# Weight subtractions hung behind their copies, phase work split around the low parts, and a later combination in a one-core attention and S5 kernel

## The chip, the core and the metric

The kernel runs on one core of a Trainium2 chip. The metric is the time of one execution on the device, in microseconds. The runs of the kernel before gave a median of 3143.69 us (3 runs, 3141.63 to 3149.01).

## What is computed

The reference is a trunk of two layers over a prompt of 1024 and a sample of 512 tokens, with 1024 channels, in float32. The kernel takes both together as 1536 tokens, 12 tiles of 128. Layer 0, with which this change deals, is attention with three head groups of different window and dilation and a SiLU gate; layer 1 is a bidirectional S5 (state space) layer. For layer 0 the core is:

```python
xqkvz = h @ w_in            # h: normed and modulated x; 1024 -> 3*3*1024 + 1024
for g, (window, dil) in enumerate(((128, 1), (512, 4), (2048, 16))):
    q, k, v = rope(q_g), rope(k_g), v_g        # 16 heads of 64
    o_g, lse_g = dilated_window_attention(q, k, v, dil, radius)
w = softmax over g of lse_g                    # the combination
y = (sum_g w_g * o_g) * silu(z) @ w_out
```

This is a shortened paraphrase of the reference's loop. The S5 layer needs tables of powers of complex numbers, computed from its parameters alone; the kernel makes them during layer 0 ("prep").

## The kernel before, in words

**Units and items.** The 16 heads are taken as 8 pairs p. A unit (p, g) is the input projection of one pair in one group, with g = 3 for the gate. The order is (0,0) to (7,0), and then (p,1), (p,2), (p,3) for p = 0 to 7. A unit with g < 3 has 12 items T, one for each tile of 128 tokens; an item is 24 matmuls of 128x384 (`gemm`, L876 to L888): 8 pieces k of the contraction, and for each piece hi by hi, hi by lo and lo by hi, since every float32 factor is split into a rounded high part and the rest. A g = 3 unit has 3 items of 24 matmuls, 512 wide. Matmuls 3k to 3k+2 of an item need the weights of piece k, the second of them the low half.

**The order of work.** `Timeline` (L90 to L114) holds the items and hooks. Before each of the 24 matmuls, and at the end (slots 0 to 24), it issues the hooks that were registered for (item, slot), in the order of registration. So a slot only fixes the place of an instruction in the in-order queue of its engine; engines run as far ahead as their operands allow. A slot of 25 or more is carried into the next items.

**Stages of an item.** After item T, at slot 24, `stage_rope` multiplies q and k by cos and sin on DVE (L914, L915) and adds the parts on POOL (L898, L899). In the next item ACT copies the value's high parts at slot 3 (L941) and DVE makes the low parts at slot 7 (L894). At slot 13 PE transposes q and k (L950, L951), at slot 16 ACT copies their high parts (L963, L965), at slot 18 DVE makes the low parts, "the qk lows" (L968, L970), and POOL copies halves of kT (L974). Scores come two items later (L994, L998), then the maximum and exponential (L1021, L1024, L1009), the transposes of the exponentials (L1042, L1052, L1054), and the product with the values (L1067), added up by ACT and POOL (L1076, L1077, L1081).

**Weights of the next unit.** `w_dma` (L824) fetches a piece into one of two buffers (wraw), from SP's queue. `w_cvt` (L837 to L844) takes one of 11 buffers (whl), copies the high part on ACT (L842) and subtracts on DVE for even k and on POOL for odd k (L843). `attention` (L692 to L782) hooks copy and subtraction together, for g < 3 at slot 16 of items 2, 4, 6 (k0 to k2), at slots 5, 6, 18 and 22 of the last item T = 11 (k3 to k6), and at slot 6 of the next unit's first item (k7). The fetch of piece k+2 follows at the same slot, since it takes the buffer of piece k. A g = 3 unit gives k its slot 19 + 6k, and the fetch 20 + 6k. Sixteen units of 12 items are followed by a unit with eight pieces (seven times g = 0 by g = 0, (7,0) by (0,1), and g = 1 by g = 2 for each of the 8 pairs); those with g = 2 are followed by the gate, which has four pieces of 256 columns.

**Combination.** At the end of (p, 2) the three groups' statistics are stored and read back (`combine_load`, L1109). `combine_prep` (L1114 to L1143) makes the factors: part 0 on DVE and ACT (L1122 to L1126), part 1 on DVE (to L1134), and part 2 transposes them on PE (L1138), copies them (L1140), stores them (L1141) and fetches them spread over the partitions as f (L1152). `combine` (L1155) begins two items later by multiplying f (L1164).

**S5 tables.** `prep_hooks` (L1361) lays one eighth of the tables beside each of seven g = 0 units, (0,1), and each g = 2 unit. `prep_tab` are POOL operations of 128x512 (L1252 to L1262) at slots 8 and 19 of items 2 to 4 and 6 to 8. `prep_phase` (L1324 to L1359), with j = 0 to 6 in items 2 to 8, doubles a table of phases: part 0 is three DVE operations (L1346 to L1348), part 1 three more (L1350 to L1352), on up to 128x252 elements, all operands in SBUF.

```python
            for k in range(n):
                i, sl = [(first + 2, 16), (first + 4, 16), (first + 6, 16), (last, 5), (last, 6), (last, 18), (last, 22), (last + 1, 6)][k]
                H(i, sl, self.w_cvt, nu, k)
                ...
                if k + 2 < n:
                    H(i, sl, self.w_dma, nu, k + 2)
```

Of the kernel before, what the change touches and what calls it, by code (L numbers as in the profile page):

```python
# [10 lines left out]
F32 = mybir.dt.float32  # L11
F32R = mybir.dt.float32r
BF = mybir.dt.bfloat16
I32 = mybir.dt.int32
AF = mybir.ActivationFunctionType
ALU = mybir.AluOpType
# [11 lines left out]
NW = 11  # L28
# [112 lines left out]
class Kern:  # L141
# [157 lines left out]
    def startup(self):  # L299


        nc, I = self.nc, self.I
# [100 lines left out]
        self.s5_some(3.4)  # L403
        for T in range(2):
            self.x_scale(T)
        self.w_cvt(unit, 0, True)
        self.w_cvt(unit, 1, True)
        for i in range(8):
            if i < 3:
                piece_load(i + 5)  # L410
# [24 lines left out]
            if i in (5, 7):  # L435
                self.to_hm(None, 2, 0, S, None, (i - 3) // 2)
            for k in ((2,), (3,), (), (4,), (5,), (6,), (7,), ())[i]:
                self.w_cvt(unit, k, True)
            if i > 0:
                multiply(i - 1)  # L440
            if i < 7:
# [250 lines left out]
    def attention(self):  # L692
# [10 lines left out]
        for u, (p, g) in enumerate(units):  # L703
            first = at_unit[p, g] = len(tl.items)
            n = NT if g < 3 else 3
            for T in range(n):
# [5 lines left out]
                if g < 3:  # L712
                    end = u + 2 == len(units)
                    early = u == 0 and T == 0
                    at = {"rope": (0, 24), "qk": (2, 2) if early else divmod(38, 25), "scores": divmod(76, 25), "soft": divmod(79, 25), "et": divmod(100, 25), "pv": divmod(118, 25)}
                    if end:
                        at.update(LAST.get(T, {}))
                    end_of = 0
                    for nm, (ds_, sl) in at.items():

                        ds_, sl = at[nm] = divmod(max(25 * ds_ + sl, end_of), 25)
                        end_of = 25 * ds_ + sl + max((0, *LATER.get(nm, ()))) + 1
                        H(i + ds_, sl, getattr(self, "stage_" + nm), p, g, T)
                        for part, d in enumerate(LATER.get(nm, ())):
                            H(i + ds_ + (sl + d) // 25, (sl + d) % 25, getattr(self, "stage_" + nm), p, g, T, part + 1)
                    if T == NT - 1:
                        st = divmod(25 * at["soft"][0] + at["soft"][1] + LATER["soft"][0], 25)
                        H(i + st[0], st[1], self.stats_out, p, g)
                        if g == 0:
                            H(i + at["pv"][0] + (at["pv"][1] + LATER["pv"][1] + 1) // 25, (at["pv"][1] + LATER["pv"][1] + 1) % 25, self.u0_store, p)  # L730
                        if end:
                            H(i + st[0], st[1], self.combine_load, p)
                            for k, sl in enumerate((4, 10, 16)):
                                H(i + 3, sl, self.combine_prep, p, k)
                        elif g == 2:
                            H(i + st[0], st[1], self.combine_load, p)
                            for k, sl in enumerate((10, 16, 24)):
                                H(i + 4, sl, self.combine_prep, p, k)
                            for c in range(3):
                                for k, (ds_, sl) in enumerate(((0, 10), (0, 22), (1, 14), (1, 24))):  # L740
                                    H(i + 6 + 3 * c + ds_, sl, self.combine, p, c, k)
                            H(i + 16, 2, self.u0_load, p + 1)
                elif u + 1 < len(units) or T < n - 1:
                    H(i, 24, self.stage_silu, p, T)
            last = i
            if u + 1 == len(units):
                continue
            nu = units[u + 1]
            if g == 3:
                for k in range(8):  # L750
                    H(first + (19 + 6 * k) // 25, (19 + 6 * k) % 25, self.w_cvt, nu, k)
                    if k < 2:
                        H(first, 3, self.w_dma, nu, k)
                    if k < 6:
                        H(first + (20 + 6 * k) // 25, (20 + 6 * k) % 25, self.w_dma, nu, k + 2)
                continue
            n = 8 if nu[1] < 3 else 4
            for k in range(n):
                i, sl = [(first + 2, 16), (first + 4, 16), (first + 6, 16), (last, 5), (last, 6), (last, 18), (last, 22), (last + 1, 6)][k]
                H(i, sl, self.w_cvt, nu, k)  # L760
                if k < 2:
                    H(first, 3, self.w_dma, nu, k)
                if k + 2 < n:
                    H(i, sl, self.w_dma, nu, k + 2)

        second = at_unit[0, 1]
        starts = [12 + 11 * k for k in range(7)] + [second] + [at_unit[p, 2] for p in range(npairs)]
# [66 lines left out]
            nc.sync.dma_start(raw, W[256 * k:256 * k + 256, 9216 + 128 * p:9344 + 128 * p].rearrange("(k p) n -> p k n", p=128))  # L834
        self.raw[(unit, k)] = raw

    def w_cvt(self, unit, k, start=False):  # L837

        nc, g = self.nc, unit[1]
        raw = self.raw.pop((unit, k))  # L840
        w = self.sb(self.pools["A"], [128, 2, 384] if g < 3 else [128, 2, 2, 128], F32R, "whl", bufs=NW)
        nc.scalar.activation(w[:, 0], raw, AF.Copy)  # L842
        (nc.gpsimd if start or k in (1, 3, 5, 7) else nc.vector).tensor_tensor(w[:, 1], raw, w[:, 0].bitcast(F32), op=ALU.subtract)  # L843
        self.wt[(unit, k)] = w  # L844

    @staticmethod
    def tok_cols(g, T):
# [513 lines left out]
    def prep_hooks(self, b, i):  # L1361
# [13 lines left out]
        H(i + 9, 0, self.prep_b_out, b, 0)  # L1375
        H(i + 9, 20, self.prep_b_out, b, 1)
        for j in range(7):
            H(i + 2 + j, 18, self.prep_phase, b, j, 0)
            H(i + 2 + j, 22, self.prep_phase, b, j, 1)


    ADA = [(0, 2 * D), (0, 2 * D + 512)] + [(1, 512 * k) for k in range(6)]
# [641 lines left out]
```

## Time and profile before

| | |
|---|---|
| median of the runs | 3143.69 us (3141.63 to 3149.01) |
| the profiled execution's own time | 3140.71 us |
| its span in the profile | 3138.9 us |
| mean granted TensorE clock | 0.976 of full speed |
| TensorE (PE) busy | 89% |
| VectorE (DVE) busy | 68% |
| ScalarE (ACT) busy | 54% |
| GpSimd (POOL) busy | 52% |

The profile is one execution. The busy shares are means over stages: start to about 55 us, the g = 0 units to 792, (0,1) to 893.6, (0,2) to 973.2, then seven rounds of g = 3, 1, 2 to 2251, and the rest of the program, with the S5 layer, to the end. In a row of a timeline the first number is the start in us from the beginning of the span and the second the duration; "x6" is the number of like instructions drawn together, and the bracket gives the idle time of the engine before the row and what ended it.

### The profile page before, as it was taken

The numbers are of one execution on the slowest core, as the hardware profiler recorded it, in microseconds if no ns is written. First come the engines' busy times: TensorE is split into PE (matmuls) and PEld (weight loads), VectorE is DVE, ScalarE is ACT, GpSimd is POOL, SyncE is SP. The second block draws the span as 40 slices with busy tenths as digits, with TensorE's granted clock in tenths as the row PEclk, the third lists the DMA queues.
The fourth block names the chain that finished last, engine by engine and source line by source line (L and its number), as shares of the span: only waits on it lengthen the run. The fifth ranks groups of instructions, "written<-read, shape, count | busy, mean of one in ns | idle before, by whom it ended". The sixth has DMA issues, their size and how long they took to land. (4 is left out here: it accounts for less than half of the span.)

```text
span 3138.9 us, 52520 instructions
## 1 busy us (share of the span) xinstructions
PE 2788.1 (89%) x16181; PEld 2419.8 (77%) x16181; DVE 2131.3 (68%) x6071; ACT 1700.8 (54%) x5120; POOL 1620.9 (52%) x2657
## 2 busy tenths in 40 slices
PE   6799999998898888888888888889899989889998
PEld 5788888887787878878787887878678666667887
DVE  7777777776875766657575766757654799984345
ACT  5867666677665665656565665656544222223221
POOL 3655555554754554545464554545464466552343
PEclk8999999999899999999999999999999999999999
DMA  7122222221222222221222212222444555436553
GB/s 207 47 76 86 85 80 83 73 86 49 61 69 57 62 51 60 55 67 42 73 54 54 67 44 60 53 62 58 132 138 121 166 186 163 153 132 178 171 154 128
DMA packets 428232, 293.78 MB, mean 94 GB/s; under 512 B 140288, under 2 KB 379152, under 8 KB 427824
## 3 DMA queue, kind: packets, MB, share of 16 engines
q1 hardware_dynamic: 427808, 290.16, 32.3%
q8 instruction: 129, 2.11, 0.3%
q14 instruction: 151, 1.24, 0.1%
q10 hardware_dynamic: 144, 0.26, 0.0%
HBM read 204.72 MB, written 85.62 MB: 92 GB/s over the span
## 5 line engine op out<-in xcount | busy, mean ns | idle before, releaser
L885 PE MATMUL mm<-whl,hp 128*128 128x384 f32 x4584 | 992.0, 353 | 5.1 <-ACT hp L356 2.8
L885 PEld LDWEIGHTS mm<-whl,hp 128*128 128x128 f32 x4584 | 804.1, 196 | 22.2 <-issue 12.0
L885 PE MATMUL mm<-whl,hs 128*128 128x384 f32 x2304 | 498.6, 350 | 0.0
L885 PEld LDWEIGHTS mm<-whl,hs 128*128 128x128 f32 x2304 | 398.1, 192 | 7.5 <-issue 7.2
L968 DVE SCALAR_TENSOR_TENSOR qT<-qkT,qT 64x128 fp32r<-64x128 f32 x576 | 166.4, 289 | 304.1 <-ACT kT L965 297.9
L974 POOL CAST kT<-kT 64x128 fp32r<-64x128 f32 x576 | 171.2, 297 | 316.9 <-ACT kT L965 297.3
L1654 PE MATMUL mm<-hp,wi 128*128 128x512 f32 x1104 | 279.4, 401 | 2.6 <-ACT sig L1691 2.6
L1009 ACT ACTIVATE e<-e,st 128x128 f32<-128x128 f32 (+2 forms) x576 | 249.3, 434 | 52.4 <-DVE st L1024 48.4
L1081 POOL TENSOR_TENSOR u<-u,pw 128x128 f32<-128x128 f32 x384 | 188.7, 491 | 167.8 <-ACT u L1077 152.1
L950 PE MATMUL qkT<-ident,t 128*128 128x128 f32 x288 | 89.5, 311 | 184.4 <-POOL t L899 182.3
L1654 PEld LDWEIGHTS mm<-hp,wi 128*128 128x128 f32 x1104 | 202.7, 188 | 53.7 <-issue 8.6
L963 ACT ACTIVATE qT<-qkT 64x128 fp32r<-64x128 f32 x576 | 155.9, 271 | 153.6 <-PE qkT L951 146.2
L1076 ACT ACTIVATE pw<-pv 64x256 f32<-64x256 f32 x576 | 217.5, 378 | 36.2 <-PE pv L1067 25.5
L898 POOL TENSOR_TENSOR t<-t,t 128x128 f32<-128x128 f32 x288 | 137.8, 478 | 187.2 <-DVE t L915 180.2
L950 PEld LDWEIGHTS qkT<-ident,t 128*128 128x128 f32 x288 | 40.7, 141 | 241.5 <-POOL t L899 238.5
L941 ACT ACTIVATE vs<-mm 64x128 fp32r<-64x128 f32 (+1 forms) x350 | 95.6, 273 | 225.6 <-DVE t L915 223.0
L843 POOL TENSOR_TENSOR whl<-wraw,whl 128x384 fp32r<-128x384 f32 (+1 forms) x116 | 113.8, 981 | 139.9 <-ACT whl L842 138.5
L843 DVE TENSOR_TENSOR whl<-wraw,whl 128x384 fp32r<-128x384 f32 (+1 forms) x108 | 85.0, 787 | 138.5 <-ACT whl L842 138.0
L970 DVE TENSOR_TENSOR kT<-qkT,kT 64x128 fp32r<-64x128 f32 x576 | 166.3, 289 | 9.8
L1054 DVE TENSOR_TENSOR et<-eT,et 128x512 fp32r<-128x512 f32 (+1 forms) x288 | 163.5, 568 | 6.6 <-ACT et L1052 6.3
L1081 POOL TENSOR_TENSOR U<-U,pw 128x128 f32<-128x128 f32 x192 | 90.7, 472 | 147.6 <-ACT U L1077 140.1
L1067 PE MATMUL pv<-et,vs 128*128 128x256 f32 x704 | 147.8, 290 | 19.6 <-DVE et L1054 17.6
(368 smaller groups left out, 6395.0 us busy)
## 6 DMA issues: line engine op xcount, KB each, us to landing
wraw<-in_attn_w_in SPq DMA_DIRECT2D x192, 192.0 KB
par<-par_d SPq DMA_DIRECT2D x64, 512.0 KB
f<-f_d SPq DMA_DIRECT2D x44, 384.0 KB
par_d<-zs SPq DMA_DIRECT2D x64, 256.0 KB
U<-in_ada_w SPq DMA_DIRECT2D x16, 768.0 KB
par_d<-f SPq DMA_DIRECT2D x64, 128.0 KB
raw<-in_ssm_w_in SPq DMA_DIRECT2D x14, 512.0 KB
u_d<-u SPq DMA_DIRECT2D x8, 768.0 KB
```

Of the source, the lines that this page charges most:

```text
L843: (nc.gpsimd if start or k in (1, 3, 5, 7) else nc.vector).tensor_tensor(w[:, 1], raw, w[:, 0].bitcast(F32), op=ALU.subtract)
L885: nc.tensor.matmul(ps[:, :384], self.hv(a, k, self.tok_cols(g, T)), self.wt[((p, g), k)][:, b], start=m == 0, stop=m == 23)
L963: nc.scalar.activation(qT[r, h], tp[r, 0:128], AF.Copy, scale=-0.125)
L968: nc.vector.scalar_tensor_tensor(qT[o, h], tp[r, 0:128], -0.125, qT[r, h].bitcast(F32), op0=ALU.mult, op1=ALU.subtract)
L970: nc.vector.tensor_tensor(kT[r, 1, h, c], tp[r, 128:256], kT[r, 0, h, c].bitcast(F32), op=ALU.subtract)
L974: nc.gpsimd.tensor_copy(kT[o, 0, h, c], kT[r, 0, h, c].bitcast(F32))
L1009: nc.scalar.activation(e[:, h, :W], e[:, h, :W], AF.Exp, scale=-1.0, bias=st[:, T, h, 0:1], accum_out=st[:, T, h, 1:2])
L1054: nc.vector.tensor_tensor(et[:, 1, 0:n], tp[:, 0:n], et[:, 0, 0:n].bitcast(F32), op=ALU.subtract)
L1067: nc.tensor.matmul(pv[:, h], V[key][:, 2 * h:2 * h + 2].rearrange("p a c -> p (a c)"), et[:, :, ci, h], start=ci == 0, stop=ci == len(chun ...
L1076: nc.scalar.activation(w[hi], pv[hi, h], AF.Copy)
L1081: nc.gpsimd.tensor_tensor(u, u, w[:, a], op=ALU.add)
L1654: nc.tensor.matmul(st["ps"], state[("w", u)][a][:, k], self.hv(b, k, slice(512 * c, 512 * c + 512)), start=m == 0, stop=m == 23)
```

## The change

The helper that copies and subtracts a piece of weights is split in two parts, the copy (part 0) and the subtraction (part 1). At start both are still called together, all subtractions on POOL. In a unit with g < 3, k0 to k2 are copied at slot 16 of items 2, 4, 6 as before, and subtracted at slot 10 of the item behind. With L the first slot of the last item, k3 to k7 are copied at L + 4, 7, 19, 22 and 34 (before: 5, 6, 18, 22 and 31), and subtracted at L + 9, 12, 24, 27 and 39. In a g = 3 unit the copies come at 15 + 7k and the subtractions at 19 + 7k. The fetch of piece k+2 is issued behind the subtraction of piece k.

The three parts of the combination's factors, at slots 10, 16 and 24 of one item, come at slots 10 and 20 of it and 10 of the next. The phase parts, at slots 18 and 22, come at 9 and 20.

```diff
--- before.py
+++ after.py
@@ -403,8 +403,8 @@
         self.s5_some(3.4)
         for T in range(2):
             self.x_scale(T)
-        self.w_cvt(unit, 0, True)
-        self.w_cvt(unit, 1, True)
+        self.w_cvt(unit, 0)
+        self.w_cvt(unit, 1)
         for i in range(8):
             if i < 3:
                 piece_load(i + 5)
@@ -435,7 +435,7 @@
             if i in (5, 7):
                 self.to_hm(None, 2, 0, S, None, (i - 3) // 2)
             for k in ((2,), (3,), (), (4,), (5,), (6,), (7,), ())[i]:
-                self.w_cvt(unit, k, True)
+                self.w_cvt(unit, k)
             if i > 0:
                 multiply(i - 1)
             if i < 7:
@@ -734,8 +734,8 @@
                                 H(i + 3, sl, self.combine_prep, p, k)
                         elif g == 2:
                             H(i + st[0], st[1], self.combine_load, p)
-                            for k, sl in enumerate((10, 16, 24)):
-                                H(i + 4, sl, self.combine_prep, p, k)
+                            for k, sl in enumerate((110, 120, 135)):
+                                H(i + sl // 25, sl % 25, self.combine_prep, p, k)
                             for c in range(3):
                                 for k, (ds_, sl) in enumerate(((0, 10), (0, 22), (1, 14), (1, 24))):
                                     H(i + 6 + 3 * c + ds_, sl, self.combine, p, c, k)
@@ -746,22 +746,20 @@
             if u + 1 == len(units):
                 continue
             nu = units[u + 1]
+
             if g == 3:
-                for k in range(8):
-                    H(first + (19 + 6 * k) // 25, (19 + 6 * k) % 25, self.w_cvt, nu, k)
-                    if k < 2:
-                        H(first, 3, self.w_dma, nu, k)
-                    if k < 6:
-                        H(first + (20 + 6 * k) // 25, (20 + 6 * k) % 25, self.w_dma, nu, k + 2)
-                continue
+                at_w = [(15 + 7 * k, 19 + 7 * k) for k in range(8)]
+            else:
+                L = 25 * (last - first)
+                at_w = [(66, 85), (116, 135), (166, 185), (L + 4, L + 9), (L + 7, L + 12), (L + 19, L + 24), (L + 22, L + 27), (L + 34, L + 39)]
             n = 8 if nu[1] < 3 else 4
             for k in range(n):
-                i, sl = [(first + 2, 16), (first + 4, 16), (first + 6, 16), (last, 5), (last, 6), (last, 18), (last, 22), (last + 1, 6)][k]
-                H(i, sl, self.w_cvt, nu, k)
                 if k < 2:
                     H(first, 3, self.w_dma, nu, k)
+                for part in range(2):
+                    H(first + at_w[k][part] // 25, at_w[k][part] % 25, self.w_cvt, nu, k, part)
                 if k + 2 < n:
-                    H(i, sl, self.w_dma, nu, k + 2)
+                    H(first + at_w[k][1] // 25, at_w[k][1] % 25, self.w_dma, nu, k + 2)
 
         second = at_unit[0, 1]
         starts = [12 + 11 * k for k in range(7)] + [second] + [at_unit[p, 2] for p in range(npairs)]
@@ -834,14 +832,17 @@
             nc.sync.dma_start(raw, W[256 * k:256 * k + 256, 9216 + 128 * p:9344 + 128 * p].rearrange("(k p) n -> p k n", p=128))
         self.raw[(unit, k)] = raw
 
-    def w_cvt(self, unit, k, start=False):
+    def w_cvt(self, unit, k, part=None):
 
         nc, g = self.nc, unit[1]
-        raw = self.raw.pop((unit, k))
-        w = self.sb(self.pools["A"], [128, 2, 384] if g < 3 else [128, 2, 2, 128], F32R, "whl", bufs=NW)
-        nc.scalar.activation(w[:, 0], raw, AF.Copy)
-        (nc.gpsimd if start or k in (1, 3, 5, 7) else nc.vector).tensor_tensor(w[:, 1], raw, w[:, 0].bitcast(F32), op=ALU.subtract)
-        self.wt[(unit, k)] = w
+        raw = self.raw[unit, k]
+        if part != 1:
+            w = self.wt[(unit, k)] = self.sb(self.pools["A"], [128, 2, 384] if g < 3 else [128, 2, 2, 128], F32R, "whl", bufs=NW)
+            nc.scalar.activation(w[:, 0], raw, AF.Copy)
+        if part != 0:
+            w = self.wt[(unit, k)]
+            (nc.gpsimd if part is None or k in (1, 3, 5, 7) else nc.vector).tensor_tensor(w[:, 1], raw, w[:, 0].bitcast(F32), op=ALU.subtract)
+            del self.raw[unit, k]
 
     @staticmethod
     def tok_cols(g, T):
@@ -1375,8 +1376,8 @@
         H(i + 9, 0, self.prep_b_out, b, 0)
         H(i + 9, 20, self.prep_b_out, b, 1)
         for j in range(7):
-            H(i + 2 + j, 18, self.prep_phase, b, j, 0)
-            H(i + 2 + j, 22, self.prep_phase, b, j, 1)
+            H(i + 2 + j, 9, self.prep_phase, b, j, 0)
+            H(i + 2 + j, 20, self.prep_phase, b, j, 1)
 
 
     ADA = [(0, 2 * D), (0, 2 * D + 512)] + [(1, 512 * k) for k in range(6)]
```

## Rows read from the trace of the kernel before

**Rows 1.** the page, section 1: span, and busy time of TensorE
```profile
span 3138.9 us, 52520 instructions
...
PE 2788.1 (89%) x16181; PEld 2419.8 (77%) x16181; DVE 2131.3 (68%) x6071; ACT 1700.8 (54%) x5120; POOL 1620.9 (52%) x2657
```

**Rows 2.** busy time in stretches, core 0: us, PE (x), PEld, DVE, ACT, POOL, PEclk, DMA, GB/s
```profile
55.00:792.00 737.00, 652.91 (x4229) 585.38 (x4227) 543.46 (x1778) 523.17 (x1587) 409.76 (x739) 0.97 0.26 73
...
973.20:2251.00 1277.80, 1116.34 (x6725) 1023.95 (x6724) 836.67 (x2832) 786.96 (x2647) 652.35 (x1246) 0.98 0.23 57
```

**Rows 3.** waits over the whole span: engine, line, releaser: us in total, times, longest
```profile
PE qkT L950 <- POOL t L899: 182.3, 149, 3.3
...
DVE whl L843 <- ACT whl L842: 138.0, 85, 5.1
```

**Rows 4.** groups of PE, 973.2 to 2251: busy us, mean ns, idle before, releasers
```profile
L950 PE MATMUL qkT<-ident,t 128*128 128x128 f32 x169 | 52.4, 310 | 117.8 <-POOL t L899 117.1
...
L1138 PE MATMUL qkT<-ident,cd 128*72 128x128 f32 x8 | 2.8, 350 | 18.9 <-DVE cd L1134 18.9
```

**Rows 5.** waits of PE, 55 to 792
```profile
PE qkT L950 <- POOL t L899: 46.6, 46, 3.2
...
PE sc L998 <- DVE kT L970: 16.8, 15, 3.3
```

**Rows 6.** timeline of DVE, item T7 of (3,2): start, us, operation, [idle before, releaser]
```profile
1486.40 0.59 DVE L968 SCALAR_TENSOR_TENSOR qT<-qkT,qT 64x128 fp32r<-64x128 f32 x2 [1.30 <-ACT kT L965]
...
1487.61 0.57 DVE L1346 TENSOR_TENSOR f<-f,p_pb 128x128 f32<-128x128 f32 x1
...
1489.63 0.29 DVE L1352 TENSOR_TENSOR f<-f 128x128 f32<-128x128 f32 x1
```

**Rows 7.** timeline of POOL, the same item
```profile
1484.66 1.29 POOL L1256 TENSOR_TENSOR zs<-zs 128x512 f32<-128x512 f32 x1
```

**Rows 8.** timeline of PE, the same item
```profile
1491.77 0.33 PE L950 MATMUL qkT<-ident,t 128*128 128x128 f32 x1 [1.69 <-POOL t L899]
```

**Rows 9.** timeline of DVE: subtractions at the boundary (3,1) to (3,2) and in its T2
```profile
1431.65 1.42 DVE L843 TENSOR_TENSOR whl<-wraw,whl 128x384 fp32r<-128x384 f32 x1
...
1437.05 0.56 DVE L843 TENSOR_TENSOR whl<-wraw,whl 128x384 fp32r<-128x384 f32 x1 [2.22 <-ACT whl L842]
...
1453.08 0.43 DVE L843 TENSOR_TENSOR whl<-wraw,whl 128x256 fp32r<-128x256 f32 x1 [2.15 <-ACT whl L842]
```

**Rows 10.** timeline of POOL, the boundary (3,1) to (3,2)
```profile
1431.64 1.01 POOL L843 TENSOR_TENSOR whl<-wraw,whl 128x384 fp32r<-128x384 f32 x1
...
1439.82 0.45 POOL L899 TENSOR_TENSOR t<-t,t 128x128 f32<-128x128 f32 x1
```

**Rows 11.** timeline of SP's queue, the same boundary: the fetch of k7
```profile
1437.13 0.37 SPq L831 DMA_DIRECT2D wraw<-in_attn_w_in  x1
```

**Rows 12.** timeline of ACT, the same boundary: the copy of k7
```profile
1439.62 0.52 ACT L842 ACTIVATE whl<-wraw 128x384 fp32r<-128x384 f32 x1 [0.65 <-DMA wraw<-in_attn_w_in]
```

**Rows 13.** timeline of PE, the same boundary: the last six matmuls of T0
```profile
1441.72 1.21 PE L885 MATMUL mm<-whl,hp 128*128 128x384 f32 x6
```

**Rows 14.** timelines of PE and POOL at the boundaries to (6,0) and (7,2)
```profile
607.09 2.12 PE L885 MATMUL mm<-whl,hp 128*128 128x384 f32 x6
...
2155.61 0.46 POOL L899 TENSOR_TENSOR t<-t,t 128x128 f32<-128x128 f32 x1
...
2157.51 1.21 PE L885 MATMUL mm<-whl,hp 128*128 128x384 f32 x6
```

**Rows 15.** busy time in stretches, behind L950 at two boundaries (columns of rows 2)
```profile
1258.00:1261.40 3.40, 3.40 (x14) 3.40 (x13) 1.16 (x4) 2.86 (x13) 1.58 (x3) 0.51 0.48 54
...
1440.40:1443.80 3.40, 3.40 (x23) 3.37 (x24) 1.76 (x6) 3.17 (x13) 1.72 (x4) 1.00 0.33 51
```

**Rows 16.** timelines of SP's queue and DVE: factors of the combination of p = 3
```profile
1543.42 0.34 SPq L1141 DMA_DIRECT2D f_d<-ft  x1
...
1551.17 1.10 DVE L1164 TENSOR_TENSOR f<-f,u 128x512 f32<-128x512 f32 x1 [1.13 <-DMA f<-f_d]
```

## The prediction

> **What bounds the kernel now.** I read the busy shares first. TensorE works 2788.1 us, 89% of a span of 3138.9 [rows 1], so some 351 us of its idle time is all that a reordering can win. The table by stages says where it idles: 84 us from 55 to 792, where the g = 0 units run, 161 us in the seven rounds of g = 1, 2, 3 from 973 to 2251 [rows 2]. Nothing of the change lies behind 2251. The list of waits then names the last releaser. PE waits 182.3 us before the qk transposes L950 for the rope sum on POOL (L899), and DVE stands 138.0 us in front of its weight subtractions L843 until ACT has made the copy [rows 3]. The second is a wait of an engine that isn't the bound and counts only where something that PE needs is queued behind it. So I read PE alone, by stage. Of the 117.8 us before L950 in the rounds, and 18.9 before the combine transpose L1138 [rows 4], most lie in g = 2 units; in the g = 0 stage it is 46.6 before L950 and 16.8 before the scores for the low half of kT on DVE [rows 5].
>
> One item of (3,2) shows the loop. DVE makes the qk lows from 1486.40, then six phase operations from 1487.61 to 1489.92, and only then rope [rows 6]; POOL sums; PE gets L950 at 1491.77 after 1.69 us idle [rows 8]. The loop L950, ACT copies, lows, phase, rope, sum is longer than PE's own item by just that. DVE had waited 1.30 us ahead of the lows [rows 6], and the change moves phase work into that gap.
>
> **Phase work moved (prep_phase part 0 to slot 9, part 1 to slot 20).** It runs in ten items of each g = 2 unit, of seven g = 0 units and of (0,1). In the item shown 2.31 us stand between lows and rope. Part 0 took about 1.65 of it and part 1 .85. Part 1 stays behind the lows, part 0 goes before them. If part 0 fits into the gap of 1.30 the loop loses up to that. What speaks against the full gain: POOL's table operations hold slots 8 and 19, the first of this item 1.29 us from 1484.66 [rows 7]. Part 0's first operation (two SBUF inputs) took .57 beside such an operation, and part 1's last .29 when POOL was free [rows 6]. The same shows in the subtractions: .56 alone at 1437.05, 1.42 at 1431.65 beside POOL's own of 1.01 at 1431.64 [rows 9, 10]. At slot 9 part 0 starts half a microsecond into the first table operation, at slot 20 part 1 runs beside the second and POOL's additions behind it, so part 1 is now the long one (1.65 instead of .85) and part 0 spills some .4 us over the gap: in this item about 0 is won (1.65 - .80 - .85), in the item behind, with 128x252 operands, about .6. In T5, without a table operation, nothing stalls today.
>
> The Trainium skill, "SBUF — State Buffer", section "Who interferes with whom", says that a DVE instruction with two SBUF inputs contends with a GpSimd instruction that reads SBUF, and that the other fully blocks. The trace agrees as far as 1.42 = .56 + most of 1.01 goes; taken strictly over a whole part it makes a rival below.
>
> **Subtractions moved (w_cvt part 1).** In T2 of this unit DVE stands 2.15 us for the copy and subtracts .43 (1453.08) right ahead of the lows [rows 9]. The copy stands behind ACT's own qk copies, so the lows come .46 later than they could, the step to the next operation counted. After the change the subtraction comes ten slots behind the lows, in time that DVE has. I take .75 in T2 and .85 in T6 together with their small phase operations.
>
> Sum for a g = 2 unit: -.75 (T2), +.1 (T3, POOL's subtraction nearer the rope), -.85 (T6), 0 (T7), -.6 (T8): -2.1, by eight units -17, and 1 us of clock (below): **-18**. Bounds: .5 per unit (only the subtractions) and 6.3 (all that moves is hidden in T2, T3, T6, T7 and T8: 1.36 + .81 + 1.54 + 1.3 + 1.3, each the smaller of the time moved and the stall that is there), thus -4 and -50.
> In g = 0 units the lows freed of the subtraction take away most of the scores' 16.8 [rows 5], I take 11, and phase the same share of 46.6 as 18 + 7 are of 117.8 (21%): 10. **-21**; bounds -10 and -31. In g = 1 units no phase work runs, the subtractions are freed in front of the lows of T4 and T6: .9 each, **-7** (bounds -3 and -9). (0,1): **-2** (0 to -5).
>
> **Combination later.** Part 0 stays at (4,10), part 2 (L1138) goes from (4,24) to (5,10). Its wait of 18.9 [rows 4] shrinks as PE first does ten matmuls more. But f, which DVE needs at L1164, comes 7.75 us after the store L1141 (1543.42 to 1551.17) and is already waited for there by 1.13 [rows 16]. L1140 and L1141 now stand behind rope and value lows on DVE, some .8 us later, and PE arrives earlier: what is saved at L1138 is waited for two items later, DVE's lows behind L1164. With the subtraction of k0 gone from that item and about 1 us less in g = 3 units, where the subtraction held the et lows, I take **0** (bounds -8 and +8).
>
> **What it costs: the last weights of the next unit.** Only two wraw buffers exist, so piece k7 is fetched after k5's subtraction, which goes from slot 18 of the last item to slot 24, on POOL behind L1081 and L898/L899. Before: issue at 1437.13, copy at 1439.62 (2.49 later) to 1440.14, subtraction to 1441.24, needed by the 22nd and 23rd of the 24 matmuls of the next T0, the fourth and fifth of six from 1441.72, at 1442.2 and 1442.4 [rows 10 to 13]: 1.2 us spare. After: L899 ends 1440.27, subtraction to 1441.28, issue 1441.31, copy 1443.80 to 1444.32, subtraction from 1444.40 to 1445.41 [durations of rows 10 to 12]. PE waits 3.0 us for k7's low half, and the stall before L950 at this boundary is not taken away, since L898 stands behind POOL's L1081 as before. The same working for sixteen boundaries with eight pieces (g = 0 to 0 seven times, to (0,1), and to g = 2 eight times): eight lose 2.7 to 3.0, seven .9 to 2.2, and the one at 602 nothing, because PE comes to its six matmuls only at 607.09 [rows 14]; the last, from 2155.61 and 2157.51 [rows 14], is again 3.0. Sum 34; **+33** for what the sums ahead gain there. Bounds +15 (POOL takes the subtraction into the gap before L1081 after all) and +48. SP's prep loads come 4.2 us later behind k7's issue; they are wanted at (1,11) of the next unit and just in time.
>
> **Clock.** A stall can leave PE at the lower level: of two such boundaries, the 3.4 us behind the L950 stall ran at .51 (1.2 GHz) from 1258.0 and at 1.00 from 1440.4 [rows 15]. One such stretch costs up to 1.7 us. Four to five of the sixteen new stalls: **+8** (0 to 27).
>
> The span's own execution took 3140.7; -18 - 21 - 7 - 2 + 0 + 33 + 8 = -7, so 3133.7. The median of the runs stands 3.0 above this execution: 3136.7, and I write **3136**. The measurement can tell 0.2%, 6.3 us.
>
> **Rivals.** (B) POOL's operations don't slow the phase parts as I take it: gains of 50 + 31 + 7 + 2 = 90 against 41, -49: 3095 on the same basis. For it: DVE waits 1.30 in front of the lows; against: .57 against .29 in [rows 6]. (C) slower, by k7 alone: as PE gains elsewhere it comes earlier to the 22nd matmul while k5's subtraction stays tied to L1081, so all sixteen cost 3.0, and each is followed by a slow stretch of 1.6: 16 x 4.6 = 74 against 48, +26: 3170. It decides from 3.0 us per boundary (48 / 16). (D) the lock taken strictly: moved phase parts wait out POOL's operation whole, and nothing of the phases is won. Left are the subtractions: 7 + 11 + 7 = 25 against 41, +16: 3160. That is what the page "SBUF — State Buffer" of the Trainium skill would give. (E) the change does nothing to PE, since what it moves are waits of engines with room and k7 comes in time: 3144, inside the forecast's own range.
>
> **How the numbers follow.** Forecast .45, with 3122 to 3150 as its own range, from which .23 falls below 3137.4 and .22 within 0.2%; B .20; C .20; D .15. Faster .43, same .22, slower .35. The range reaches to the other cases: 3096 to 3168.
>
> **What would show it.** In the changed profile: a PE wait at L885 on POOL's or ACT's whl late in T0 of each g = 0 and g = 2 unit (3 us if right, none if wrong); DVE's 138 us before its subtractions near 0; the L950 stall of T8 and T9 in g = 2 units by half a microsecond smaller (B: nearly gone; D: unchanged); L1346 to L1352 of part 1 near .55 each; L1138's wait smaller and L1164's wait for f larger. The forecast is wrong if k7 is in time, or if L950 loses more than 60 us.

## The result and the profile after

The changed kernel took 3059.76 us (median of 4 runs, 3058.81 to 3061.17) against 3142.66 for the kernel before in the runs made beside it: a ratio of 0.9736, with an interval of 0.9717 to 0.9756. It is 83 us faster, where 7 us were forecast, and lies below the range. One execution of the first experiment's kernel took 13964.61 us at a granted clock of 0.172, and that kernel's time below is the median of its three others.

The page of the changed kernel, section 1, beside [rows 1]. All lines behind the edit have moved by one, so L951 is what L950 was.

```profile
span 3058.6 us, 52458 instructions
...
PE 2774.0 (91%) x16181; PEld 2418.3 (79%) x16181; DVE 2158.9 (71%) x6071; ACT 1699.5 (56%) x5120; POOL 1626.3 (53%) x2657
```

The span is 80.3 us shorter, and TensorE's busy time 14 us less. The stages, beside [rows 2]:

```profile
54.30:756.90 702.60, 647.62 (x4228) 587.28 (x4227) 544.24 (x1776) 523.04 (x1587) 408.08 (x738) 0.96 0.27 77
...
929.50:2173.50 1244.00, 1110.82 (x6728) 1023.26 (x6725) 859.42 (x2833) 786.88 (x2649) 657.18 (x1246) 0.98 0.24 59
```

From 54 to 757 PE idles 55 us (before 84), from 929.5 to 2173.5 it is 133 (before 161). The waits, beside [rows 3], and PE's groups in the second stretch, beside [rows 4]:

```profile
PE qkT L951 <- POOL t L900: 128.0, 111, 3.2
...
DVE whl L844 <- ACT whl L841: 38.5, 30, 3.9
```

```profile
L951 PE MATMUL qkT<-ident,t 128*128 128x128 f32 x169 | 52.6, 311 | 94.2 <-POOL t L900 83.7 <-DVE ft L1141 9.1
...
L999 PE MATMUL sc<-kT,qT 128*128 128x192 f32 x224 | 35.5, 276 | 15.2 <-DVE kT L971 15.2
...
L1139 PE MATMUL qkT<-ident,cd 128*72 128x128 f32 x8 | 2.4, 299 | 10.4 <-DVE cd L1135 10.4
```

The wait before the qk transposes fell from 182 to 128 us, and DVE's before its subtractions from 138 to 38. L1139 waits 10.4 us where it was 18.9, but the scores L999 now wait 15.2 for DVE's low half of kT (9.0 before), and 9.1 of the 94.2 us before L951 end with a copy of the combination. Before, in the same stretch:

```profile
PE sc L998 <- DVE kT L970: 9.0, 14, 1.1
```

In the g = 0 stage of the changed kernel, beside [rows 5], both waits are down:

```profile
PE qkT L951 <- POOL t L900: 32.1, 28, 3.2
...
PE sc L999 <- DVE kT L971: 6.8, 7, 2.5
```

Item by item, each item's length compared between the two traces, the 80 us lie as follows (some 3 of them at the start and behind the attention; where an item is taken to begin moves each figure by up to 1 us). The items behind the first of the g = 2 units are about 43 us shorter in all, those of the g = 0 units about 43, T4 to T7 of the g = 1 units 19, the last of the g = 3 units 9. Longer are the first items of the g = 0 and g = 2 units, by 14, and T0 to T3 of the g = 1 units, by 23.

**The boundary.** The same boundary as in [rows 9 to 13], in the changed kernel: DVE, SP, ACT, POOL and PE of the timeline.

```profile
1377.17 0.56 DVE L844 TENSOR_TENSOR whl<-wraw,whl 128x384 fp32r<-128x384 f32 x1 [1.67 <-ACT whl L841]
...
1377.76 0.37 SPq L829 DMA_DIRECT2D wraw<-in_attn_w_in  x1
...
1380.35 0.53 ACT L841 ACTIVATE whl<-wraw 128x384 fp32r<-128x384 f32 x1 [0.50 <-DMA wraw<-in_attn_w_in]
...
1380.01 0.45 POOL L900 TENSOR_TENSOR t<-t,t 128x128 f32<-128x128 f32 x1
...
1380.42 1.96 POOL L844 TENSOR_TENSOR whl<-wraw,whl 128x384 fp32r<-128x384 f32 x2
...
1380.52 0.48 PE L951 MATMUL qkT<-ident,t 128*128 128x128 f32 x1 [3.15 <-POOL t L900]
...
1383.03 1.44 PE L886 MATMUL mm<-whl,hp 128*128 128x384 f32 x6
```

The fetch of k7 goes out at 1377.76. POOL makes k5's subtraction, the first of the two at 1380.42, only 2.7 us later. The fetch did not wait for it: it follows DVE's subtraction of k6 (1377.17 to 1377.73). The compiled program says the same. These are, from its list of instructions, the fetches of k5, k6 and k7 of the first such boundary with the semaphores each waits for, before and after:

```
57 L831 DMA wraw_1828<-in_attn_w_in 128x3x128 [waits DMAHW5_49,Pool_49]
58 L831 DMA wraw_1835<-in_attn_w_in 128x3x128 [waits DMAHW3_49,DMAHW1_49,DVE_49]
59 L831 DMA wraw_1875<-in_attn_w_in 128x3x128 [waits DMAHW4_49,DMAHW2_49,Pool_49]
...
57 L829 DMA wraw_1839<-in_attn_w_in 128x3x128 [waits DMAHW5_49,Pool_49]
58 L829 DMA wraw_1845<-in_attn_w_in 128x3x128 [waits DMAHW3_49,DMAHW1_49,DVE_49]
59 L829 DMA wraw_1896<-in_attn_w_in 128x3x128 [waits DMAHW4_49,DMAHW3_49,DVE_49]
```

Before, k7 waits for POOL and for the queue that brought k5: it takes k5's buffer. After, it waits for DVE and for the queue that brought k6. So it is at all sixteen boundaries to a unit with eight pieces, and the addresses of the buffers agree. By the order of the hooks in the source k5's buffer would be the one; but in the compiled program the subtraction of k6 stands ahead of the fetch, and that of k5 behind it. Over the whole span PE waits for a weight in these matmuls once, for .4 us:

```profile
PE mm L886 <- POOL whl L844: 0.4, 1, 0.4
```

### The profile page after: what moved, and what is told of

The parts are those of the page before. It is cut to its first block, busy times and chain, and to the rows that moved or that the text cites. A ratio compares the mean times of both kernels' runs of the same rounds, so it can differ in the third digit from the quotient of the medians.

```text
span 3058.6 us, 52458 instructions
## 1 busy us (share of the span) xinstructions
PE 2774.0 (91%) x16181; PEld 2418.3 (79%) x16181; DVE 2158.9 (71%) x6071; ACT 1699.5 (56%) x5120; POOL 1626.3 (53%) x2657
## 5 line engine op out<-in xcount | busy, mean ns | idle before, releaser
L975 POOL CAST kT<-kT 64x128 fp32r<-64x128 f32 x576 | 177.4, 308 | 323.3 <-ACT kT L966 303.9
L951 PE MATMUL qkT<-ident,t 128*128 128x128 f32 x288 | 88.5, 307 | 139.0 <-POOL t L900 128.0
L951 PEld LDWEIGHTS qkT<-ident,t 128*128 128x128 f32 x288 | 40.8, 142 | 189.1 <-POOL t L900 187.4
L1053 ACT ACTIVATE et<-eT 128x512 fp32r<-128x512 f32 (+1 forms) x288 | 144.6, 502 | 44.3 <-PE eT L1043 33.5
L841 ACT ACTIVATE whl<-wraw 128x384 fp32r<-128x384 f32 (+1 forms) x224 | 112.7, 507 | 89.3 <-DMA wraw<-in_attn_w_in 86.5
```

The lines of the kernel that those rows point to most:

```text
L975: nc.gpsimd.tensor_copy(kT[o, 0, h, c], kT[r, 0, h, c].bitcast(F32))
L1053: nc.scalar.activation(et[:, 0, 0:n], tp[:, 0:n], AF.Copy)
```

## The experiments

**One part at a time.** The first kernel has only the phase edit:

```diff
-            H(i + 2 + j, 18, self.prep_phase, b, j, 0)
-            H(i + 2 + j, 22, self.prep_phase, b, j, 1)
+            H(i + 2 + j, 9, self.prep_phase, b, j, 0)
+            H(i + 2 + j, 20, self.prep_phase, b, j, 1)
```

> The kernel before with the phase parts alone moved, from slots 18 and 22 to 9 and 20. Theory 1 (the changed trace is read item by item): the phase work accounts for most of what the g = 2 units won behind T2 and for about half of the g = 0 units' gain, some 27 + 20 us, so 40 to 52 us faster than before, and the stall before the qk transposes of T8 and T9 in g = 2 units near 1.3 and 1.2 us instead of 1.7 and 2.1, with the slow stretch of T9 gone. Rival (the prediction's step): POOL's table operations give the moved parts back what they save, 10 to 20 us. Rival (shared lock, strictly): no gain over 5 us.

Measured: 3079.92 us, ratio 0.9798 (0.9772 to 0.9823), 62 us faster than before (3142.18): more than any theory had. The item of [rows 6 to 8] in this kernel, DVE, POOL and PE of the timeline:

```profile
1438.42 1.07 DVE L1346 TENSOR_TENSOR f<-f,p_pb 128x128 f32<-128x128 f32 x1
...
1439.41 0.28 DVE L1347 TENSOR_TENSOR f<-f,p_pb 128x128 f32<-128x128 f32 x1
...
1440.06 0.59 DVE L968 SCALAR_TENSOR_TENSOR qT<-qkT,qT 64x128 fp32r<-64x128 f32 x2
...
1441.27 0.31 DVE L1350 TENSOR_TENSOR f<-f,p_pb 128x128 f32<-128x128 f32 x1
...
1442.09 0.50 DVE L1352 TENSOR_TENSOR f<-f 128x128 f32<-128x128 f32 x1
...
1438.05 1.29 POOL L1256 TENSOR_TENSOR zs<-zs 128x512 f32<-128x512 f32 x1
...
1439.60 0.64 POOL L974 CAST kT<-kT 64x128 fp32r<-64x128 f32 x2 [0.26 <-ACT kT L965]
...
1444.44 0.33 PE L950 MATMUL qkT<-ident,t 128*128 128x128 f32 x1 [0.98 <-POOL t L899]
```

Part 0 begins .37 us into POOL's table operation, and its first operation takes 1.07 instead of about .28: it ends at 1439.49, just behind POOL's at 1439.34. The second runs at .28 and the third, behind it, at .30, and the lows begin at 1440.06. POOL's own copy of kT, released by the same ACT copies as the lows, starts at 1439.60, .46 before the lows. In the kernel before it started .20 before them, at 1486.20 against 1486.40 [rows 6]:

```profile
1486.20 0.64 POOL L974 CAST kT<-kT 64x128 fp32r<-64x128 f32 x2 [0.25 <-ACT kT L965]
```

So part 0 runs over DVE's wait by some .26. Behind the lows stands only part 1, 1.32 us from 1441.27 to 1442.59, where 2.31 us stood before. PE's stall is .98 instead of 1.69. The g = 0 stage of this kernel, PE's waits beside [rows 5]:

```profile
PE qkT L950 <- POOL t L899: 26.9, 28, 3.2
...
PE sc L998 <- DVE kT L970: 16.7, 15, 3.3
```

The 46.6 us before L950 are 26.9; the scores' wait is untouched, as it should be.

The second kernel is the complement: the split of copy and subtraction, with phase and combination as before.

```diff
-            for k, sl in enumerate((110, 120, 135)):
-                H(i + sl // 25, sl % 25, self.combine_prep, p, k)
+            for k, sl in enumerate((10, 16, 24)):
+                H(i + 4, sl, self.combine_prep, p, k)
...
-            H(i + 2 + j, 9, self.prep_phase, b, j, 0)
-            H(i + 2 + j, 20, self.prep_phase, b, j, 1)
+            H(i + 2 + j, 18, self.prep_phase, b, j, 0)
+            H(i + 2 + j, 22, self.prep_phase, b, j, 1)
```

(against the changed kernel)

> The kernel before with the split of copy and subtraction alone, at the slots of the changed kernel; phase and combination as before. Theory 1: what is left when phase and combination are taken out of the changed kernel: g = 1 units win at T4, T5 and T7 some 2.4 us each, g = 3 units 1.1, g = 2 and g = 0 units 1 to 1.5 each, less some 14 us at the first item of each unit: 35 to 50 us faster than before. The fetch of k7 is held by no POOL work. Rival (the prediction's step): each of sixteen boundaries loses up to 3 us waiting for k7 and the split alone is 0 to 20 us slower than before.

Measured: 3099.66 us, ratio 0.9869 (0.9840 to 0.9899), 42.5 us faster. PE's waits in its g = 0 stage:

```profile
PE qkT L951 <- POOL t L900: 53.2, 47, 3.4
...
PE sc L999 <- DVE kT L971: 7.6, 8, 2.5
```

Here it is the scores' wait that falls, 16.8 to 7.6, and L950's that doesn't. In the g = 0 stage the two edits release different waits. Together they would give 105 us, and the changed kernel has 83. By the items of the traces, what is missing lies in three places, and other items give a little of it back. In T9 of the g = 2 units it is 7.6 us: the split shortens that item alone, but not beside the phase edit. In T0 to T3 of the g = 1 units it is 19 us, and only 4 with the combination's factors back (the next kernel). In the first items of the g = 0 units it is 7 us, and no run shows why.

The third kernel takes the combination's factors back in the changed kernel (the first half of the diff above).

> The changed kernel with the combination's three parts back at slots 10, 16 and 24 of one item. Theory 1: the later combination only moves the wait: in the changed trace T0 of the g = 1 units wins 8 us in all, T1 loses 12 and T3 19. With the parts back, 10 to 22 us faster than the changed kernel, and the waits before L951 on the copied factors (9 us) gone. Rival (the later place is part of the gain, as the wait before the transpose, 18.9 us, falls to 9): 5 to 15 us slower than the changed kernel. Rival (the wait of DVE for f decides in both): within 4 us of it.

Measured: 3055.98 us, ratio 0.9721 (0.9699 to 0.9744), against 0.9736 for the changed kernel: no difference that can be told, where this run's own theory had 10 to 22. The place of the factors is worth nothing that shows in the whole, as forecast. By the items the g = 1 units are 11.6 us shorter with the factors back; the items of the other units are 9 us longer, 5 of it in first items, where no edit reaches, and the cause of that is not shown. A part of what moves in the g = 1 units is clock: by length and granted clock of the items, T1 lost 10 us to the lower level in the kernel before and 2 in the changed one, and T3 nothing before and 15 after. Where the wait goes in the changed kernel is seen in these events of (3,1), DVE, PE, SP, DVE and PE in order of time:

```profile
1305.87 0.29 DVE L1141 COPY ft<-qkT 72x128 f32<-72x128 f32 x1
...
1306.30 0.30 PE L951 MATMUL qkT<-ident,t 128*128 128x128 f32 x1 [1.51 <-DVE ft L1141]
...
1306.18 0.34 SPq L1142 DMA_DIRECT2D f_d<-ft  x1
...
1313.90 1.03 DVE L1165 TENSOR_TENSOR f<-f,u 128x512 f32<-128x512 f32 x1 [2.72 <-DMA f<-f_d]
...
1315.89 0.68 PE L999 MATMUL sc<-kT,qT 128*128 128x192 f32 x3 [2.26 <-DVE kT L971]
```

The copy of the factors (L1141) stands behind rope and the value lows on DVE until 1305.87. PE's next qk transposes wait 1.51 us for it, since they take the same PSUM bank (tag qkT has one). The store follows at 1306.18, f is there at 1313.90, DVE has stood 2.72 us for it, and the scores, whose low half of kT is queued behind, 2.26.

**The buffer of k7.** The two buffers pinned, even pieces in one and odd in the other, in the changed kernel:

```diff
-        raw = self.sb(..., "wraw", **(slot or {"bufs": 2}))[:, 0:384]
+        raw = self.sb(..., "wraw", **(slot or {"bufs": 1, "tag": "wraw%d" % (k % 2)}))[:, 0:384]
```

> The changed kernel with the two wraw buffers pinned, even pieces in one and odd pieces in the other, so that k7 must be fetched behind k5's subtraction on POOL as the prediction had it; in the changed kernel the fetch takes the buffer of k6, freed by DVE. Theory 1: the prediction's working of the boundary was right and only the buffer wrong: waits of up to 3 us on PE at the last matmuls of the first item of the g = 0 and g = 2 units, 25 to 45 us slower than the changed kernel. Rival: the boundary has room that I did not see, within 6 us of it.

Measured: 3102.46 us, ratio 0.9866 (0.9844 to 0.9889), 43 us slower than the changed kernel. The boundary to (3,2) in this kernel, POOL, SP, ACT and PE, and PE's waits over its span:

```profile
1406.17 0.45 POOL L900 TENSOR_TENSOR t<-t,t 128x128 f32<-128x128 f32 x1
...
1406.58 1.01 POOL L844 TENSOR_TENSOR whl<-wraw,whl 128x384 fp32r<-128x384 f32 x1
...
1407.61 0.37 SPq L829 DMA_DIRECT2D wraw<-in_attn_w_in  x1
...
1410.14 0.52 ACT L841 ACTIVATE whl<-wraw 128x384 fp32r<-128x384 f32 x1 [4.14 <-DMA wraw<-in_attn_w_in]
...
1410.72 0.45 PE L886 MATMUL mm<-whl,hp 128*128 128x384 f32 x1 [1.70 <-ACT whl L841]
...
1411.79 0.62 PE L886 MATMUL mm<-whl,hp 128*128 128x384 f32 x2 [0.62 <-POOL whl L844]
```

```profile
PE mm L886 <- ACT whl L841: 20.9, 14, 3.1
...
PE mm L886 <- POOL whl L844: 8.3, 14, 0.6
```

L900 ends at 1406.62, the subtraction at 1407.59, the fetch goes out at 1407.61, the copy ends at 1410.66, and PE stands 1.70 us for k7's high half and .62 for the low, 2.3 in all. These are the steps that the prediction worked out (with 3.0 at their end), for a buffer that the changed kernel doesn't use. Over the span it is 20.9 + 8.3 = 29.2 us of waits. Most of the other 14 lie in the second items of the same units, which are 13 us longer, 11 of it by the lower clock.

**Which phase part, and what POOL's operations cost.** Part 0 alone at slot 9, part 1 left at 22, in the kernel before (one line of the first diff):

> The kernel before with phase part 0 alone moved to slot 9; part 1 stays at slot 22. Theory: DVE's wait of 1.3 us ahead of the qk lows covers part 0 up to .4 us even where its first operation waits for POOL's table operation, and part 1, already behind the lows, has nothing to win by going from slot 22 to 20: 50 to 65 us faster than before, within 6 us of the kernel with both parts moved. Rival: part 1's new place counts too: under 45 us faster.

Measured: 3088.26 us, ratio 0.9819 (0.9798 to 0.9840), 59.8 us faster beside its own runs of before (3148.01). Its interval overlaps that of the first kernel: part 0 is the whole of it within what can be told.

Then the phase edit without most of POOL's table operations, and its base:

```diff
         for k in range(6):
-            H(i + 2 + k // 2, (8, 19)[k % 2], self.prep_tab, 0, k)
+            if k in (0, 3):
+                H(i + 2 + k // 2, (8, 19)[k % 2], self.prep_tab, 0, k)
```

(and the same for the second table)

> The kernel before with four of six of POOL's table operations left out of each half of the S5 tables (the second, third, fifth and sixth), so that the tables hold only first products; none then runs beside the phase parts of T3's first slot, T4, T7's first slot and T8. It is the base for the next run. Expected 10 to 35 us faster than the kernel before, since part 0 no longer takes .57 us for an operation that takes .28 alone.

> The same with the phase parts moved to slots 9 and 20. Theory (DVE's wait ahead of the lows covers part 0, whether its first operation is held by POOL or not): the move is worth 45 to 65 us here too, against the run with few tables, as it was 61 us with all of them. Rival (the prediction's step: POOL gives back much of what the move saves): without the tables the move is worth clearly more, over 75 us. Rival (most of the gain was that the phase parts left POOL's operations): clearly less, under 35 us.

Measured: 3110.22 us (ratio 0.9889, 0.9866 to 0.9913) and 3058.61 (0.9722, 0.9703 to 0.9740). The kernel before is 36 us faster without the operations (3146.42 in the runs beside it), at the edge of what was expected. The move is worth 51.6 us without them and 62 with them. The first phase operation, L1346, over the span, in the order before, phase edit, base with few tables, phase edit with few tables (columns as in [rows 4]):

```profile
L1346 DVE TENSOR_TENSOR f<-f,p_pb 128x4 f32<-128x4 f32 (+6 forms) x112 | 49.4, 441 | 4.3 <-POOL f L1336 1.9
```

```profile
L1346 DVE TENSOR_TENSOR f<-f,p_pb 128x4 f32<-128x4 f32 (+6 forms) x112 | 64.5, 576 | 15.1 <-POOL f L1336 14.7
```

```profile
L1346 DVE TENSOR_TENSOR f<-f,p_pb 128x4 f32<-128x4 f32 (+6 forms) x112 | 36.8, 329 | 4.2 <-POOL f L1336 1.8
```

```profile
L1346 DVE TENSOR_TENSOR f<-f,p_pb 128x4 f32<-128x4 f32 (+6 forms) x112 | 31.7, 283 | 15.3 <-POOL f L1336 14.9
```

Moved, the operation costs 15 us more in all with the tables (49.4 to 64.5) and 5 less without them (36.8 to 31.7). So POOL does hold it. In the item of [rows 6 to 8] that costs PE nothing, since DVE would have waited; the stall before L950 is .96 with few tables, where it was .98 with all of them:

```profile
1428.57 0.33 PE L950 MATMUL qkT<-ident,t 128*128 128x128 f32 x1 [0.96 <-POOL t L899]
```

The mean over the eight g = 2 units is .98 here and .97 with all tables. One item later, with operands of 128x252, it is .56 against 1.16, so there the table operations do cost PE .6, and by the ratios the phase edit with few tables is 24 us faster than the one with all of them. In the base the phase operations stand between lows and rope, in PE's loop, and the six take 196 us in all with few tables and 215 with all. POOL's own queue, freed of table operations, is a rival for the 36 us, but a small one: in the g = 0 and g = 2 units L898 starts .53 us behind the end of L915 on average with few tables, and .56 with all. What else makes up the 36 is not shown.

**What is left.** A third buffer, pieces fetched one further ahead, in the changed kernel (five value buffers instead of six give the room):

```diff
-        raw = self.sb(..., "wraw", **(slot or {"bufs": 2}))[:, 0:384]
+        raw = self.sb(..., "wraw", **(slot or {"bufs": 3}))[:, 0:384]
...
-                if k < 2:
+                if k < 3:
...
-                if k + 2 < n:
-                    H(first + at_w[k][1] // 25, at_w[k][1] % 25, self.w_dma, nu, k + 2)
+                if k + 3 < n:
+                    H(first + at_w[k][1] // 25, at_w[k][1] % 25, self.w_dma, nu, k + 3)
...
-                    V[key] = self.sb(A, [128, 4, 64], F32R, "vs", bufs=6)
+                    V[key] = self.sb(A, [128, 4, 64], F32R, "vs", bufs=5)
```

> The changed kernel with a third wraw buffer and pieces k0 to k2 fetched ahead, piece k+3 behind the subtraction of k; for its room the value tiles have 5 buffers instead of 6. Theory: what is left at the first item of the g = 0 and g = 2 units (2.2 us before L951 in each, and slow stretches behind some) is ACT standing for k5 and k6 in front of the copies that POOL's L1082 adds, so with the pieces there early most of it goes: 20 to 45 us faster than the changed kernel. Rival (POOL and the order of the additions hold it, whenever the weights come): within 6 us. Rival (a fetch earlier means that ACT is held by its wait for a free weight buffer instead): within 6 us, with ACT waiting for PE at L841.

> The changed kernel with 5 value buffers instead of 6, as a control for the kernel with three wraw buffers: same time within 6 us if the sixth isn't needed, slower if ACT or PE wait for values.

Measured: 3014.60 us (0.9579, 0.9564 to 0.9595), by the ratios 49 us faster than the changed kernel; the control with five value buffers alone 3065.39 (0.9741, 0.9716 to 0.9766), the same as it. ACT's wait for weights in the changed kernel and in this one:

```profile
ACT whl L841 <- DMA wraw<-in_attn_w_in: 86.5, 70, 5.0
```

```profile
ACT whl L841 <- DMA wraw<-in_attn_w_in: 29.4, 24, 2.3
```

The gain is not only where it was expected. The first items of the g = 0 and g = 2 units give 18 to 19 us, T0 and T1 of the g = 1 units 29 to 30: behind a gate unit, too, ACT stood for weights. The stall before L951 in the first item of g = 2 units falls only from 2.2 to 1.6.

The combination one item later, `i + 7` for `i + 6` in its hooks. Its second multiplication then reads sums to which the next pair has begun to add.

> The changed kernel with the combination itself one item later (from the eighth item behind the g = 2 unit's end instead of the seventh). Theory: in the changed kernel DVE stands at L1165 for the factors f, with the qk lows behind it, and PE's T3 of the g = 1 units pays 2.3 us per unit and a slow stretch; a later multiplication leaves f time to land: 10 to 25 us faster than the changed kernel, the waits of the scores for kT (17 us) gone. Rival (DVE's own work, 1.1 us of L1165, then holds another item's lows): within 6 us.

Measured: 3056.55 us, ratio 0.9712 (0.9679 to 0.9746). By the ratios that is 7 us faster than the changed kernel, but the intervals overlap, and its runs lie between 3044.30 and 3063.40. In the profiled execution T3 of the g = 1 units is 40 us shorter in all, as the theory has it; T5, T7 and T10 are 37 longer, as the rival has it, and T6 and T9 28 shorter. In sum the g = 1 units are 22 us shorter, and 8 of that are lost in the g = 2 units.

Last, two kernels with three buffers and the subtractions of k0 and k2 at slot 10 of items 4 and 10 (`at_w = [(66, 110), (116, 135), (166, 260), ...`). One starts the combination twelve slots later, the other has the factors back at their old slots:

> The changed kernel with three wraw buffers and pieces fetched ahead, five value buffers, the combination twelve slots later (behind the qk lows of its item, not an item later), and the DVE subtractions of k0 and k2 put at slot 10 of items 4 and 10, where the loop has room. Theory: f is no longer waited for in front of lows, some 15 to 25 us, and the subtractions .4 us each in T3 and T8 loops, some 4: 15 to 30 us faster than the kernel with three buffers alone (3015). Rival: the g = 1 units' own loop takes the stall over: within 8 us of it.

> The same with the combination's factors back at slots 10, 16 and 24 and the combination itself where it was. Theory: with the weights there early PE stands at T0 for the factors instead of at T3 for f: within 10 us of the kernel with three buffers alone. Rival: the earlier factors save a wait that their later place only moved: 10 to 25 us faster than that kernel.

Measured: 2997.25 us (0.9528, 0.9508 to 0.9548) and 2996.64 (0.9523, 0.9507 to 0.9539). By the ratios both are 16 to 18 us faster than with three buffers alone, and 149 us faster than before, the best of this study. The second's theory had it within 10 us; its rival, that the earlier factors save a wait, is nearer. Each changes two things at once, and no run parts them. The page of the second:

```profile
span 2998.5 us, 52473 instructions
...
PE 2748.3 (92%) x16181; PEld 2395.5 (80%) x16181; DVE 2165.7 (72%) x6071; ACT 1699.6 (57%) x5120; POOL 1621.1 (54%) x2657
```

## Why the prediction was wrong, by its own steps

**What bounds the kernel**, and the way to read it, held: PE's stalls before L950, the loop of lows, phase, rope and sum, and DVE's gap ahead of the lows. The failure is in the sum.

**The boundary (+33, and +8 of clock).** The step that failed is "piece k7 is fetched after k5's subtraction". Made true in the pinned kernel, it gives waits for k7 of 29 us where 34 were summed, and 43 us in all where the two terms held 41. That the last two are so near is in part luck: the 43 stand beside the changed kernel, whose first items are longer already. With the buffer that the program takes, PE waits .4 us for k7 in the whole run. The first items still cost 14 us: the stalls before L951 in them, which did stay, grow by 5 us, and by length and granted clock they lose 20 us to the lower level instead of 13. So some 27 us of the error come of reading the holder of a buffer from the source order; the compiled program names it.

**Phase work (in the -18 and -21).** This is the second step that failed, "in this item about 0 is won". Part 0 was foreseen at 1.65 us and took 1.07 + .28 + .30. The error is in how it was booked: "1.65 - .80 - .85" charges part 1's old .85, which stands in the loop before and after, in place of the .4 of part 0 that runs over. Also, 1.65 and .85 are sums of durations that overlap; by their starts the two parts are 1.50 and .81 of the 2.31. With what the first run showed it is 2.31 before, less 1.32 of part 1 behind the lows, less the .26 that runs over: .73, and the stall fell by .71. The .6 of T8 became 1.0. The stretch at the lower clock behind T9's stall, put at 1 us per kernel, which six of the eight units had, is gone in all: T9 went from 9.04 us to 6.93 on average, of which .97 is stall. In the g = 0 units I scaled by a share (21% of 46.6); the run gave 42%. Phase work was worth 62 us alone, where the terms held about 20: of the single steps this is the costliest.

**Subtractions.** For the scores I took 11 us, and 16.8 fell to 6.8. In g = 1 units 7 were taken and T4 to T7 gave 19; the et lows of the g = 3 units gave 9, which I had set against the combination. The split alone was worth 42.5 us.

**Combination (0).** Nothing that shows in the whole, by the path forecast: what L1138 won, L1164 waited for. The wait for the bank of the transposes was not foreseen.

**The rivals.** (B) came nearest in time, 3095, and is right that the gap ahead of the lows covers part 0; its condition, that POOL doesn't slow the parts, is false. (D): the Trainium skill, "SBUF — State Buffer", section "Who interferes with whom", calls the shared port pair an exclusive lock, and the trace agrees: part 0's first operation took 1.07 us and ended .15 behind POOL's. The time that was drawn from it, 3160, doesn't follow, as only one of the three operations meets POOL's and DVE had the time. (C) shares the forecast's late k7, which the pinned kernel shows at 43 us where (C) had 74, and has no place in the changed one. (E) is right that k7 comes in time; that the change does nothing to PE is refuted by the 83 us.

Open: why the compiled program puts k6's subtraction first, what lengthens the first items beside stall and clock, and why the gains of phase and split don't add up there.

## What to carry to other kernels

Before a wait is priced from the source, look in the compiled program for the semaphore that the instruction waits for: with rotating buffers the holder can change with an edit that only moves an instruction on another engine. Work that a lock stretches is free while it lies in time in which its engine waits for something else; count it by its end against that wait's end, not by its own length. Shortening a stall that is followed by a stretch at the lower clock can give back twice what is taken off it: in T9, 2.1 us for 1.0.

## What was not expected of the hardware

Behind T9's stall of 2.1 us PE ran at the lower of its two levels in six of the eight g = 2 units of the kernel before; with a stall of 1.17 it stayed at the upper one in all eight, and that alone was 9 us. It is not the length alone: the boundary stall of 2.79 us was followed by 1.00 [rows 15], the one of 3.15 at the same place in the changed kernel by .56 (columns of [rows 2]):

```profile
1380.50:1383.90 3.40, 3.38 (x13) 3.39 (x14) 1.16 (x4) 2.00 (x7) 2.46 (x4) 0.56 0.26 31
```

One transposed block of 72 rows, whose copy stood late in DVE's queue, cost the next transposes 1.51 us in the unit shown and 9.1 in six units, since they share a bank.
